# Router logits from four 32-column groups of the array, with the weights stationary

## The chip, the cores and the metric

The kernel runs on one core of one Trainium2 chip. The metric is the device time of one execution in microseconds. The engines are named as in the profile: PE is the matrix engine's products, PEld its weight loads, DVE the vector engine, ACT the scalar engine, POOL the general-purpose engine, and SP the engine whose queue issues most DMA transfers.

## The reference

One transformer block over 1024 tokens of width 1024, batch 1, float32. The mixing half feeds the residual stream; the second half routes tokens to experts. What the change touches is the router, the line of `aff`:

```
x = x + g1 * mixed                                  # (1024, 1024)
h2 = rmsnorm(x, norm_ffn_g) * (1.0 + sc2) + sh2
aff = softmax(h2 @ w_router)                        # (1024, 16)
g, idx = top_k(aff.T, cap)                          # 16 experts, 128 tokens each
...                                                 # gate, up, silu, down for each expert
x = x + g2 * scatter_add(...)
```

## The kernel before

The kernel has three stages. The first computes the modulation and the input projection. The second runs windowed attention and the Fourier branch, and beside them, as filler, the output projection. The third runs the experts, whose weights stream in.

Tokens are handled in eight tiles of 128 rows. `oproj(t)` makes the residual stream `x2` of tile `t` from the output projection (three float32r products per pair of slices: `mm3`, L81 to L83, into `pj` or, for the last two tiles, `lg`). It then hands over to `tail(t)`, a generator that runs while the next tile is projected:

- `x2_flip` (L826, L827) transposes `x2` on PE, four 128x128 blocks into a PSUM tile `pt`, and ACT copies them to `x2T`. Two flips make a tile: `x2T[:, kc, :]` holds 128 channels by 128 tokens, for eight slices `kc`.
- L837 forms the logits: eight products, one for each `kc`, that accumulate `p[tokens, 16]`. The tokens `x2T[:, kc, :]` are stationary (128 columns), and the router's weights `wrG[:, kc, :]` move past them, 16 columns wide.
- DVE scales and shifts them (`lg`, L839), takes the maximum (`mx`, L841), ACT makes the exponentials (`ex`, L844), and DVE normalises (L846, L847) into `aff`. A sorter on DVE picks thresholds from `aff` while later tiles run.

`router_prep` computes once `wrG`, the router's weights times the norm's scale (L866), and `cb`, the constant that the shift contributes.

The output projection is spread over attention's units. In the profile L685 and L686 are attention's logits, L688 their eviction on DVE, L697 the exponentials on ACT, L714 the transposes of the probabilities, L716 their copy `pT` on ACT, L727 the products with the values (`yp`, 64 columns of the array each, two halves of 64), and L660 the transposes of the queries.

`pt()` gives one of two PSUM buffers that flips, probability transposes, query transposes and the router share. A new use waits until the one before last has been read.

The order of instructions on each engine comes from a scheduler that places them by its own estimates, except where `in_order` pins a stretch to program order. This second stage isn't pinned. The last tile's tail, L800 to L847 near 405 to 413 us, has nothing of the output projection left beside it; the selection of the first expert's tokens (`choose`, L1141 to L1178), the one-hot rows (L1242), the gather of tokens (L1250, L1259) and the first expert's products (L1228) follow.

In the first stage `part_row` (L127) already uses column groups: a stationary tile of 32 columns, `c_act[:, j, :]`, writes partitions `32 * g` to `32 * g + 32` of a PSUM tile, with `g` going round four groups, and 256 or 512 columns of weights move past it. `mod_sum` then copies the tile with ACT (L253) and sums the groups with products against ones (L255).

Of the kernel before, what the change touches and what calls it, by code (L numbers as in the profile page):

```python
# [11 lines left out]
F32 = mybir.dt.float32  # L12
# [3 lines left out]
AF = mybir.ActivationFunctionType  # L16
OP = mybir.AluOpType
AX = mybir.AxisListType
# [7 lines left out]
NE = 16  # L26
# [19 lines left out]
def block_kernel(ctx: ExitStack, tc: tile.TileContext, t_in, out):  # L46
    nc = tc.nc
    PE, ACT, DVE, POOL, SP = nc.tensor, nc.scalar, nc.vector, nc.gpsimd, nc.sync
# [7 lines left out]
    def pool(name, bufs=1, space=None, **kw):  # L56
        if space is None:
            return tc.tile_pool(name=name, bufs=bufs, reuse_waits="tile", **kw)
        return tc.tile_pool(name=name, bufs=bufs, space=space, **kw)
# [4 lines left out]
    def spacer(p, n):  # L64
        if n:
            p.tile([128, n // 4], F32, name=f"spacer{next(spaced)}", bufs=1)
# [6 lines left out]
    def pt(name="pt"):  # L73
        return ps.tile([128, 512], F32, name=name, tag="pt", bufs=2)
# [18 lines left out]
    ident = cst.tile([128, 128], F32, name="ident")  # L93
# [47 lines left out]
    def drain(g):  # L141
        for _ in g:
            pass
# [202 lines left out]
    p = pt()  # L346
# [20 lines left out]
    def terms(ts, kc, hs_, o):  # L367
        for l, r in ((0, w_h), (1, w_h), (0, w_l)):
            for s_ in range(len(ts)):
                lhs = hs_[l][:, o + s_ * 128:o + s_ * 128 + 128]  # L370
                for acc, c0, c1 in zip(accs[s_], (0, 512, 1024), (512, 1024, 1280)):

                    first = kc == 0 and l == 0 and r is w_h and not (s_ and c0 == 1024)
                    PE.matmul(acc[:, :c1 - c0], lhs, r[kc][:, c0:c1], start=first, stop=(kc == 7 and r is w_l),  # L374
                              skip_group_check=c0 == 1024)
            yield
# [60 lines left out]
    p = terms(pair, 0, hs.pop(0), 0)  # L437
# [62 lines left out]
    for m, (t, kc0) in enumerate(seq):  # L500
# [20 lines left out]
        for a in range(4):  # L521
            project((t,), kc0 + a, hs_, a * 128)
            if m == 0 and a == 1:
                DVE.scalar_tensor_tensor(gg, qg, HD ** -0.5, kg, op0=OP.mult, op1=OP.mult)
                p = pt()
# [295 lines left out]
    def x2_flip(t, b, x2):  # L821
        if b == 0:
            x2Ts[t] = p3.tile([128, 8, 128], F32, name="x2T", bufs=1)
        p = pt()
        for k in range(4):
            PE.transpose(p[:, k * 128:k * 128 + 128], x2[:, (4 * b + k) * 128:(4 * b + k + 1) * 128], ident)  # L826
        ACT.activation(x2Ts[t][:, 4 * b:4 * b + 4].rearrange("p a b -> p (a b)"), p, AF.Copy)  # L827

    def tail(t, b0=0):
        x2, rs = x2s.pop(t)  # L830
        for b in range(b0, 2):
            x2_flip(t, b, x2)
            yield
        x2T = x2Ts.pop(t)
        p = pt()
        for kc in range(8):
            PE.matmul(p[:, :16], x2T[:, kc, :], wrG[:, kc, :], start=(kc == 0), stop=(kc == 7))  # L837
        lg = p3.tile([128, 16], F32, name="lg", bufs=2)
        DVE.scalar_tensor_tensor(lg, p[:, :16], rs, cb, op0=OP.mult, op1=OP.add)  # L839
        mx = p3.tile([128, 1], F32, name="mx", bufs=2)  # L840
        DVE.tensor_reduce(mx, lg, axis=AX.X, op=OP.max, negate=True)  # L841
        sm = p3.tile([128, 1], F32, name="sm", bufs=2)
        ex = p3.tile([128, 16], F32, name="ex", bufs=2)
        ACT.activation(ex, lg, AF.Exp, bias=mx, accum_out=sm)  # L844
        rsm = p3.tile([128, 1], F32, name="rsm", bufs=2)
        DVE.reciprocal(rsm, sm)  # L846
        after["aff"] = DVE.tensor_scalar(aff[:, t, :], ex, rsm, None, op0=OP.mult)  # L847
        ready.append(t)
        yield

    def router_prep():
        n2 = p3.tile([64, 128], F32, name="sb_", bufs=1)[:24]
        SP.dma_start(n2[0:8], md[1:2, :].rearrange("l (j p) -> (l j) p", p=128))
        SP.dma_start(n2[8:16], md[2:3, :].rearrange("l (j p) -> (l j) p", p=128))
        SP.dma_start(n2[16:24], t_in["norm_ffn_g"].rearrange("l (j p) -> (l j) p", p=128))
        p = pt()
        PE.transpose(p[:, :24], n2, ident[:24, :24])
        c2 = p3.tile([128, 24], F32, name="c2")
        DVE.tensor_copy(c2, p[:, :24])
        DVE.scalar_tensor_tensor(c2[:, 8:16], c2[:, 8:16], 1.0, c2[:, 16:24], op0=OP.add, op1=OP.mult)  # L860
        p = pt()
        for kc in range(8):
            PE.matmul(p[0:1, :16], c2[:, kc:kc + 1], wr[:, kc, :], start=(kc == 0), stop=(kc == 7))
        row = p3.tile([1, 16], F32, name="row")
        DVE.tensor_copy(row, p[0:1, :16])
        DVE.tensor_tensor(wrG, wr, c2[:, 8:16, None].to_broadcast([128, 8, 16]), op=OP.mult)  # L866
        p = pt()
        PE.matmul(p[:, :16], ones[0:1, :128], row, start=True, stop=True)
        DVE.tensor_copy(cb, p[:, :16])
# [65 lines left out]
    def wo_cut():  # L935
        k, j = divmod(next(wo_next), 2)
        split(wo_h[k][:, j], wo_l[k][:, j], wo_raw[k][:, j])
# [29 lines left out]
    po, p3 = None, None  # L967
# [18 lines left out]
    for n in range(len(units) + 2):  # L986
        if n == NSW:
            for _ in fill[0]:
                for g in lateq:
                    next(g, None)  # L990
            for g in lateq:
                drain(g)
            p_f.close()
            p_u.close()
            po = p_c.enter_context(pool("po"))
            p3 = p_c.enter_context(pool("p3", side="right"))
            sp[0] = p3
            spacer(p3, 0)
            g1_r, sh2_r, G2_r = (p3.tile([128, D], F32, name=n_) for n_ in ("g1_r", "sh2_r", "G2_r"))
            wr, wrG = (p3.tile([128, 8, NE], F32, name=n_) for n_ in ("wr", "wrG"))  # L1000
            cb = p3.tile([128, NE], F32, name="cb")
            load_x2(0)
            for i, r in enumerate((g1_r, sh2_r, G2_r)):
                SP.dma_start(r, md[i:i + 1, :].to_broadcast([128, D]))
            wo_h.append(po.tile([128, 2, D], F32R, name="woh3"))
            wo_l.append(po.tile([128, 2, D], F32R, name="wol3"))
            wo_cut()
            wo_cut()
            fill = [filler2()]
            SP.dma_start(wr, t_in["w_router"][0].rearrange("(k p) e -> p k e", p=128))  # L1010
        fg = front(*units[n]) if n < len(units) else iter(())
        bg = back(*units[n - 2]) if n >= 2 else iter(())
        next(fg, None)
        next(bg, None)
        next(fg, None)
        next(bg, None)
        next(bg, None)
        drain(fg)
        for g in lateq:
            for _ in range(9):  # L1020
                next(g, None)
        if n + 1 < len(units):
            qprep(*units[n + 1])
            tick()
        drain(bg)
# [277 lines left out]
    for b in range(2):  # L1303
        p = pt()
# [120 lines left out]
```

## Time and profile before

| what | value |
|---|---|
| median of 3 runs | 1007.59 us (1006.1 to 1008.08) |
| profiled execution, its own time | 1009.72 us |
| its span, first to last instruction | 1007.6 us |
| mean granted clock of PE | 0.971 |
| instructions | 13138 |
| PE busy | 949.8 us (94%) |
| DVE busy | 788.1 us (78%) |
| ACT busy | 627.8 us (62%) |
| POOL busy | 404.7 us (40%) |

A row of a timeline has the start and the duration in us, the engine, the line of the kernel, the operation, output and inputs by their names in the program, for PE the rows and columns of the stationary tile that are in use, the shape that moves, and how many such instructions follow each other; in brackets stands the idle time ahead of it and what ended it. A float32 product shows as two records of PE, each with a weight load of its own. A row of the chain of work has start, duration, engine, output and line. Times of a group are its total and the mean of one in ns. In a list of waits the three numbers are the total, the times, and the longest.

### The profile page before, as it was taken

The page shows a single profiled execution, that of the slowest core. Times are in us where ns is not written, and L with a number is a line of the kernel's source. Part 1 is how long each engine was busy: PE and PEld are TensorE (multiplying, and loading weights), DVE is VectorE, ACT ScalarE, POOL GpSimd, SP SyncE. Part 2 cuts the span into 40 slices and gives each one's busy share as a digit, 9 for nine tenths or more (in the row PEclk, how much of TensorE's full clock was granted, in tenths as well). Part 3 has the DMA queues.
Part 4 walks back from the last instruction along what each step waited for, and adds up shares of the span by engine and source line. Part 5 has one row for each costly group of instructions (what it writes and reads, how often), then busy time and mean ns, then how long its engine had stood idle before and what let it go on. Part 6 is the DMA issues. An engine that isn't in the chain of part 4 may idle for free.

```text
span 1007.6 us, 13138 instructions
## 1 busy us (share of the span) xinstructions
PE 949.8 (94%) x4737; PEld 747.4 (74%) x4737; DVE 788.1 (78%) x1240; ACT 627.8 (62%) x832; POOL 404.7 (40%) x236
## 2 busy tenths in 40 slices
PE   4997999979999999499899999999999999999995
PEld 2675877657777778358788888888888888888884
DVE  1346874787667787879869889988988898899894
ACT  2473533656555552136767777778777777777872
POOL 0025552200000000000257678769766976882203
PEclk9998999989999999599989999999999999999998
DMA  9967582461222228799989999999999999999912
GB/s 291 328 246 251 209 313 83 134 183 47 98 84 74 74 84 289 314 335 355 390 343 359 385 396 399 387 385 409 388 389 385 411 385 389 404 392 387 386 68 42
DMA packets 91641, 283.95 MB, mean 282 GB/s; under 512 B 8140, under 2 KB 25728, under 8 KB 91448
## 3 DMA queue, kind: packets, MB, share of 16 engines
q1 hardware_dynamic: 86712, 266.32, 69.5%
q0 software_dynamic: 4864, 16.80, 6.5%
q8 instruction: 37, 0.61, 0.2%
q14 instruction: 28, 0.23, 0.1%
HBM read 263.79 MB, written 21.40 MB: 283 GB/s over the span
## 4 chain that ended last, share of the span: by engine, by line
PE 83%; DVE 6%; POOL 3%; issue 2%; ACT 2%; DMA 1%; SPq 1%; POOLq 0%; ACTq 0%
PE pa L81 17%; PE pa L82 16%; PE pa L83 16%; PE pu L374 5%; PE yp L727 3%; PE pt L1269 3%; PE pj L81 2%; PE pj L82 2%; PE pt L714 2%; PE pj L83 2%; PE pa L1228 2%; PE pt L837 2%; PE lg L685 1%; DVE ws L123 1%; PE lg L686 1%
## 5 line engine op out<-in xcount | busy, mean ns | idle before, releaser
L87 DVE TENSOR_TENSOR wl<-raw,wh 128x2048 fp32r<-128x2048 f32 (+1 forms) x189 | 424.2, 2275 | 56.0 <-ACT wh L86 54.9
L86 ACT ACTIVATE wh<-raw 128x2048 fp32r<-128x2048 f32 (+1 forms) x189 | 355.4, 1896 | 73.7 <-PE pa L82 65.8
L1242 POOL TENSOR_SCALAR oneh<-tri_f,pos 128x128 bf16<-128x128 f32 x96 | 210.5, 2207 | 15.1 <-PE pt L1250 14.8
L81 PE MATMUL pa<-wh,t1h 128*128 128x512 f32 x384 | 151.4, 394 | 0.0
L83 PE MATMUL pa<-wl,t1h 128*128 128x512 f32 x384 | 149.5, 389 | 0.0
L82 PE MATMUL pa<-wh,t1l 128*128 128x512 f32 x384 | 149.5, 389 | 0.0
L81 PE MATMUL pa<-wh,t0h 128*128 128x512 f32 x360 | 143.5, 399 | 0.0
L82 PE MATMUL pa<-wh,t0l 128*128 128x512 f32 x360 | 141.1, 392 | 0.0
L83 PE MATMUL pa<-wl,t0h 128*128 128x512 f32 x360 | 141.1, 392 | 0.0
L800 POOL TENSOR_TENSOR rs<-ss,mhalf 128x1 f32<-128x1 f32 x8 | 4.5, 558 | 221.3 <-DVE ss L798 194.4
L1284 POOL TENSOR_TENSOR ys<-ys,g_r 128x512 f32<-128x512 f32 x30 | 54.5, 1837 | 84.9 <-ACT ys L1283 84.9
L83 PEld LDWEIGHTS pa<-wl,t1h 128*128 128x128 f32 x384 | 72.1, 188 | 15.1
L82 PEld LDWEIGHTS pa<-wh,t1l 128*128 128x128 f32 x384 | 72.2, 188 | 14.2
L81 PEld LDWEIGHTS pa<-wh,t1h 128*128 128x128 f32 x384 | 72.1, 188 | 14.2
L83 PEld LDWEIGHTS pa<-wl,t0h 128*128 128x128 f32 x360 | 68.1, 189 | 14.5
L81 PEld LDWEIGHTS pa<-wh,t0h 128*128 128x128 f32 x360 | 68.3, 190 | 13.7 <-issue 0.2
L82 PEld LDWEIGHTS pa<-wh,t0l 128*128 128x128 f32 x360 | 68.2, 190 | 13.6 <-issue 0.2
L1259 POOL DMA_INDIRECT xe<-h2d,idx x16 | 18.7, 1171 | 147.3 <-DVE gt L1256 147.2
L1287 POOL DMA_INDIRECT out_dram<-ys,idx x16 | 50.8, 3174 | 10.9 <-DVE ys L1286 6.4
L688 DVE CUSTOM_DVE_ANT_0 sb<-lg,bias,sink 128x384 f32<-128x384 f32 (+1 forms) x64 | 35.3, 579 | 17.4 <-PE pt L714 9.8
L278 ACT ACTIVATE hf<-pt,sh1c,G1c 128x128 f32<-128x128 f32 (+1 forms) x56 | 22.6, 480 | 38.7 <-PE pt L271 38.7
L374 PE MATMUL pu<-wh,hh 128*128 128x512 f32 x128 | 43.6, 423 | 2.3 <-ACT hh L86 2.2
(311 smaller groups left out, 1649.0 us busy)
## 6 DMA issues: line engine op xcount, KB each, us to landing
raw<-in_w_gate_dram SPq DMA_DIRECT2D x64, 1024.0 KB, 10.0
raw<-in_w_up_dram SPq DMA_DIRECT2D x64, 1024.0 KB, 8.5
raw<-in_w_down_dram SPq DMA_DIRECT2D x63, 1024.0 KB, 8.6
raw<-in_w_ada_dram SPq DMA_DIRECT2D x16, 1024.0 KB, 8.6
raw<-in_w_ada_dram SPq DMA_DIRECT2D x16, 512.0 KB, 8.7
xt<-in_x_dram SPq DMA_DIRECT2D x8, 512.0 KB, 5.0
raw<-in_w_out_dram SPq DMA_DIRECT2D x4, 1024.0 KB
raw<-in_x_dram SPq DMA_DIRECT2D x8, 512.0 KB
```

What stands on the lines that cost most here:

```text
L81: PE.matmul(o, lh, rh, start=start, stop=False)
L82: PE.matmul(o, ll, rh, start=False, stop=False)
L83: return PE.matmul(o, lh, rl, start=False, stop=stop)
L86: ACT.activation(hi, src, AF.Copy)
L87: return (eng or DVE).tensor_tensor(lo, src, hi.bitcast(F32), op=OP.subtract)
L374: PE.matmul(acc[:, :c1 - c0], lhs, r[kc][:, c0:c1], start=first, stop=(kc == 7 and r is w_l), skip_group_check=c0 == 1024)
L688: DVE.tensor_tensor_reduce(sb[:, :wid], lg[:, :wid], bias[:, kv * 4 + i, j0:j0 + wid], 1.0, sk[:, i:i + 1], op0=OP.add, op1=OP.max, accum_ ...
L727: PE.matmul(yp[par * 64:par * 64 + 64, :256], vf[:, b, kv * 64:kv * 64 + 64], pT[:, par * 256:par * 256 + 256], start=(bi == 0), stop=(bi ...
L1242: (POOL if t < shared else DVE).tensor_scalar(oneh[:, t, :], slots, pos[:, t, e:e + 1], None, op0=OP.is_equal)
L1269: PE.transpose(p[:, k * 128:k * 128 + 128], src[:, (4 * b + k) * 128:(4 * b + k + 1) * 128], ident)
L1284: POOL.tensor_tensor(ys[:, cs_], ys[:, cs_], g2_r[:, cs_], op=OP.mult)
L1287: POOL.indirect_dma_start(out=out2, out_offset=bass.IndirectOffsetOnAxis(ap=idx[:, :1], axis=0), in_=ys, in_offset=None, compute_op=OP.add)
```

## The change

The two operands of the router's product trade places. The weights `wrG[:, kc, :]`, widened with zeros from 16 to 32 columns, are stationary in column group `kc % 4`, and the 128 tokens of `x2T[:, kc, :]` move past them. The eight products leave four partial sums in `p`, group `g` (slices `g` and `g + 4`) in partitions `32 g` to `32 g + 32`, with experts down the partitions and tokens along the row. ACT copies `p` to a tile `gsum` in SBUF. One product with `gsum` stationary and `gsel` moving, where `gsel[p, e]` is one if `p % 32 == e`, sums the four groups and turns the result back to 128 tokens by 16 experts. `gsel` is made once on DVE, by adding up the four 32-column blocks of the identity; `wrG` is zeroed once on POOL.

```diff
@@ tail(t)
         x2T = x2Ts.pop(t)
+
         p = pt()
         for kc in range(8):
-            PE.matmul(p[:, :16], x2T[:, kc, :], wrG[:, kc, :], start=(kc == 0), stop=(kc == 7))
+            g = 32 * (kc % 4)
+            PE.matmul(p[g:g + 32, :128], wrG[:, kc, :], x2T[:, kc, :], start=(kc < 4), stop=(kc >= 4))
+        gs_ = p3.tile([128, 128], F32, name="gsum", bufs=1)
+        ACT.activation(gs_, p[:, :128], AF.Copy)
+        p = pt()
+        PE.matmul(p[:, :16], gs_, gsel[:, :16], start=True, stop=True)
         lg = p3.tile([128, 16], F32, name="lg", bufs=2)
@@ router_prep
-        DVE.tensor_tensor(wrG, wr, c2[:, 8:16, None].to_broadcast([128, 8, 16]), op=OP.mult)
+        DVE.tensor_tensor(wrG[:, :, :NE], wr, c2[:, 8:16, None].to_broadcast([128, 8, 16]), op=OP.mult)
@@ setting up the second part of stage two
-            wr, wrG = (p3.tile([128, 8, NE], F32, name=n_) for n_ in ("wr", "wrG"))
+            wr = p3.tile([128, 8, NE], F32, name="wr")
+            wrG = p3.tile([128, 8, 32], F32, name="wrG")
+            gsel = p3.tile([128, 32], F32, name="gsel")
+            POOL.memset(wrG, 0.0)
+            DVE.tensor_reduce(gsel, ident.rearrange("p (g e) -> p e g", g=4), axis=AX.X, op=OP.add)
```

In the changed file the eight products are L839, the copy is L841, the summing product L843, and `lg`, `mx`, `ex` become L845, L847, L850. In the rows below, a product's operands are written output, moving, stationary, and the shape is the stationary columns by the moving ones.

The scheduler places the rest of the second stage anew. On PE, around the router of the third tile (tile 2), the two halves of the product came apart before and stand together now:

```order
 L826 MATMUL pt<-ident,raw 128x128 x4
 L727 MATMUL yp<-pT,vf 64x256
-L837 MATMUL pt<-wrG,x2T 128x16 x4
+L839 MATMUL pt<-x2T,wrG 32x128 x8
 L727 MATMUL yp<-pT,vf 64x256
 L82 MATMUL pj<-woh_1523,yal 128x512
-L837 MATMUL pt<-wrG,x2T 128x16 x4
+L83 MATMUL pj<-wol_1526,yah 128x512
+L843 MATMUL pt<-gsel,gsum 128x16
 L714 MATMUL pt<-ident,sb 128x128 x4
```

Half of L727, L82 and L83 stand between the grouped product and the summing product.

On PE, around the router of the second tile (tile 1), before:

```order
L714 MATMUL pt<-ident,sb 128x128 x4
L837 MATMUL pt<-wrG,x2T 128x16 x8
L727 MATMUL yp<-pT,vf 64x256 x2
L714 MATMUL pt<-ident,sb 128x128 x4
L82 MATMUL pj<-woh_1523,yal 128x512
```

and of the change:

```order
L82 MATMUL pj<-woh_1523,yal 128x512
L839 MATMUL pt<-x2T,wrG 32x128 x8
L727 MATMUL yp<-pT,vf 64x256
L843 MATMUL pt<-gsel,gsum 128x16
L727 MATMUL yp<-pT,vf 64x256
L714 MATMUL pt<-ident,sb 128x128 x4
```

The summing product has moved in between the two halves of L727. Of the other tiles, tiles 2 and 3 have a half of L727 on each side of the grouped product, tile 6 has another product between the first four and the last four of L839, and in tiles 0, 4, 5 and 6 two or three products stand between L839 and L843.

On DVE, in the last tile's tail, the second half of the norm's shift (L806) stood behind `lg` and now stands ahead of it. Before:

```order
L805 SCALAR_TENSOR_TENSOR raw<-raw,rs,G_r 128x512
L839 SCALAR_TENSOR_TENSOR lg<-pt,rs,cb 128x16
L806 TENSOR_TENSOR raw<-raw,sh_r 128x512
L841 TENSOR_REDUCE mx<-lg 128x1
L846 RECIPROCAL rsm<-sm 128x1
```

and of the change:

```order
L805 SCALAR_TENSOR_TENSOR raw<-raw,rs,G_r 128x512
L806 TENSOR_TENSOR raw<-raw,sh_r 128x512
L845 SCALAR_TENSOR_TENSOR lg<-pt,rs,cb 128x16
L847 TENSOR_REDUCE mx<-lg 128x1
L852 RECIPROCAL rsm<-sm 128x1
```

L806 has moved up by one row, so `lg` and all that depends on it come behind it.

On ACT at the same place, a cut of expert weights (L86, `wh`) stood behind the last flip's copy; all four such cuts now stand ahead of it, and the copy to `gsum` follows it directly:

```order
L86 ACTIVATE wh<-raw 128x1024 x4
L793 ACTIVATE junk,ss<-raw 128x512
L827 ACTIVATE x2T<-pt 128x512
L841 ACTIVATE gsum<-pt 128x128
L850 ACTIVATE ex,sm<-lg,mx 128x16
```

The fourth cut has moved ahead of the flip, and nothing stands between the copies `x2T`, `gsum` and the exponentials.

## The prediction

> **What bounds the kernel now.** I read the page's busy line first, then three stretches of the span, then the chain of work over the stretch that the router lies in.
>
> ```profile
> PE 949.8 (94%) x4737; PEld 747.4 (74%) x4737; DVE 788.1 (78%) x1240; ACT 627.8 (62%) x832; POOL 404.7 (40%) x236
> ...
> 225.00:404.00 179.00, 178.60 (x1010) 132.35 (x1009) 133.49 (x468) 96.77 (x267) 4.53 (x9) 0.99 0.30 108
> 404.00:427.00 23.00, 10.47 (x56) 8.10 (x56) 19.73 (x80) 3.87 (x8) 2.36 (x3) 0.56 0.78 305
> 427.00:1000.00 573.00, 566.34 (x2687) 460.99 (x2686) 503.61 (x452) 418.75 (x313) 331.25 (x156) 0.99 0.95 359
> ```
>
> The columns of a stretch are its length, then busy time of PE, PEld, DVE, ACT and POOL, the granted clock, the DMA share and GB/s. From 225 to 404 us PE is busy 178.60 of 179 us at a clock of 0.99; DVE has 133 us of work and ACT 97, so both have room. Here seven of the eight router tails run. From 404 to 427 DVE is the busy one (19.73 of 23) and PE has half its clock: the last tail and the first selection. After that PE is the bound again. The chain agrees:
>
> ```profile
> by line: PE yp L727 13.9%; PE pj L81 12.7%; PE pj L82 12.2%; PE pj L83 12.0%; PE pt L714 11.5%; PE pt L837 6.9%; PE lg L685 4.9%; PE lg L686 4.1%; PE pt L826 3.4%; PE lg L81 3.2%; PE lg L82 3.2%; PE lg L83 3.1%; PE pt L660 2.2%; DVE sc L879
> ...
> 278.41 1.79 PE pt L837 x16
> ...
> 407.54 3.24 PE pt L837 x16
> ```
>
> The first row is the chain's share by line from 225 to 404 us. L837, the router product, holds 6.9% of 179 us, so 12.35 us for seven tiles, 1.76 each. That is 16 records of 0.11 us (1.79/16): each product is two records. The eighth takes 3.24 us at half clock.
>
> ```profile
> L837 PEld LDWEIGHTS pt<-wrG,x2T x112: 186/192/192, 258.3 to 396.0; 128*128 128x128 f32 x112
> L837 PE MATMUL pt<-wrG,x2T x112: 177/263/283, 258.5 to 396.1; 128*128 128x16 f32 x112
> ```
>
> Each record loads 128 columns of tokens to move 16 columns of weights past them. The load sets the 0.11 us, not the moving side. That is what the swap attacks.
>
> **Removed.** Tails 0 to 6: 12.35 us of PE, all of it on the path, since PE has no slack there.
>
> **Added: the grouped product (L839).** In the text L839 to L843 are lines of the changed file; in the profile's rows L839 is lg and L841 mx. Before has the same form in L127: 32 columns stationary, four groups in turn, float32.
>
> ```profile
> 48.97 0.63 PE L374 MATMUL pu<-wh,hl 128*128 128x512 f32 x2
> 49.44 0.28 PE L374 MATMUL pv<-wh,hl 128*128 128x256 f32 x1
> 49.65 1.92 PE L127 MATMUL px<-raw,c_act 128*32 128x512 f32 x16
> 51.50 0.73 PE L374 MATMUL pu<-wl,hh 128*128 128x512 f32 x2
> ...
> 49.65 0.16 PEld L127 LDWEIGHTS px<-raw,c_act 128*32 128x32 f32 x8 [0.25 <-issue]
> 50.10 0.13 PEld L127 LDWEIGHTS px<-raw,c_act 128*32 128x32 f32 x4 [0.30 <-issue]
> 50.53 0.13 PEld L127 LDWEIGHTS px<-raw,c_act 128*32 128x32 f32 x4 [0.30 <-issue]
> ```
>
> Eight products, 16 records, go in four bursts; the loads of the later ones start 0.43 us apart (50.10, 50.53). So four records run side by side in 0.43 us for 512 columns. 128 columns are a quarter, 0.11 a burst, 0.43 for four. The visit has a fixed part: 51.50 - 49.65 - 4 x 0.43 = 0.13 inside, 0.10 more on the next row (0.73 against 0.63), and 0.09 ahead (49.44 to 49.65 is 0.21 for 256 columns, where 512 take 0.235, half of 48.97 to 49.44); together 0.32. So 0.75 if loads hide wholly. A load of 32 columns takes as long as the shorter burst, so they may hide in part; 0.85 is my upper value, and I take 0.80, nearer to the rows as they stand.
>
> **Added: the summing product (L843).** A 128-column load and 16 moving columns, exactly L837's form: two records, 0.22 us. Seven tiles of 0.80 + 0.22 make 7.14 us.
>
> **Added: places where the order splits a visit.** L727 uses 64 columns of the array.
>
> ```profile
> 302.76 0.65 PE L727 MATMUL yp<-pT,vf 128*64 128x256 f32 x2
> 303.33 1.06 PE L837 MATMUL pt<-wrG,x2T 128*128 128x16 f32 x8
> 304.33 0.65 PE L727 MATMUL yp<-pT,vf 128*64 128x256 f32 x2
> 304.90 0.50 PE L82 MATMUL pj<-woh,yal 128*128 128x512 f32 x1
> ...
> 280.13 0.65 PE L727 MATMUL yp<-pT,vf 128*64 128x256 f32 x4
> 280.71 0.66 PE L714 MATMUL pt<-ident,sb 128*128 128x128 f32 x4
> ```
>
> Four records together take 0.58 us (280.13 to 280.71); two alone take 0.57 as well (302.76 to 303.33). In tile 1 the summing product now stands between L727's halves, which stood together: +0.57. Tiles 2 and 3 had them apart and keep that. Tile 6 has L839 in two visits: +0.32. Elsewhere the new order shuffles attention and output-projection rows but adds none; I price that at nothing, since PE's rows stay the same and PE always had a next one.
>
> **Added: the wait for the copy (L841).** PE cannot issue past the summing product while it waits, so all of PE's queue stands behind it.
>
> ```profile
> L385 ACT ACTIVATE kk<-pv 128x128 f32<-128x128 f32 x5 | 1.4, 285 | 0.0
> ...
> 301.67 0.66 PE L714 MATMUL pt<-ident,sb 128*128 128x128 f32 x4
> 302.43 0.60 ACT L716 ACTIVATE pT<-pt 128x512 f32<-128x512 f32 x1 [0.31 <-PE pt L714]
> ...
> 298.43 0.39 PE L83 MATMUL pj<-wol,yh 128*128 128x512 f32 x1
> 298.66 0.39 PE L81 MATMUL pj<-woh,yh 128*128 128x512 f32 x1
> ```
>
> The copy is 0.29 us (L385, same shape, from PSUM); PE's end to ACT's start is 0.10 (302.33 to 302.43). With L839's own tail (0.16: the records of L83 and L81 last 0.39 at a spacing of 0.23) and a hand-back that I put at half of ACT's 0.10, 0.60 us pass. The cover is what the order puts between: in tiles 2 and 3 half of L727 and two products, over 1 us; in tiles 0, 4, 5 and 6 two or three products, 0.56 or more with the 0.10 of leaving the visit; in tile 1 half of L727, with two pT copies of 0.60 ahead in ACT's queue. I allow 0.1 for six tiles and 0.3 for tile 1: 0.9, between zero and 0.60 each (4.2). ACT itself is early:
>
> ```profile
> ACT pT L716 <- PE pt L714: 27.6, 23, 3.5
> ```
>
> From 225 to 400 us ACT waited 27.6 us for PE in 23 places ahead of pT alone.
>
> **Sum for tiles 0 to 6:** 7.14 + 0.57 + 0.32 + 0.9 = 8.93 added, 12.35 removed, 3.42 us gained. Prologue: the memset of wrG has the size of c_act's, 0.31 us on POOL; the reduction to 32 elements lies between the next two DVE rows by elements read, near 0.3 us. Neither engine is on the path there; zero. The wider wrG holds the same 16 written columns; zero.
>
> ```profile
> L107 POOL MEMSET c_act<- 128x256 f32 x1 | 0.3, 312 | 0.3 <-POOLq L1414 0.3
> L290 DVE TENSOR_REDUCE qs<-ws 128x10 f32<-128x640 f32 x8 | 6.5, 814 | 2.9 <-ACT ws L288 2.9
> L841 DVE TENSOR_REDUCE mx<-lg 128x1 f32<-128x16 f32 x8 | 1.3, 162 | 0.1
> ```
>
> **The last tile** is latency:
>
> ```profile
> 407.33 3.43 PE L837 MATMUL pt<-wrG,x2T 128*128 128x16 f32 x16
> 407.57 0.60 ACT L827 ACTIVATE x2T<-pt 128x512 f32<-128x512 f32 x1
> 408.07 1.05 ACT L86 ACTIVATE wh<-raw 128x1024 fp32r<-128x1024 f32 x1
> 408.89 0.75 DVE L805 SCALAR_TENSOR_TENSOR raw<-raw,rs,G_r 128x512 f32<-128x512 f32 x1 [0.75 <-POOL rs L800]
> 410.80 0.23 DVE L839 SCALAR_TENSOR_TENSOR lg<-pt,rs,cb 128x16 f32<-128x16 f32 x1 [1.16 <-PE pt L837]
> 410.95 0.68 DVE L806 TENSOR_TENSOR raw<-raw,sh_r 128x512 f32<-128x512 f32 x1
> 411.55 0.16 DVE L841 TENSOR_REDUCE mx<-lg 128x1 f32<-128x16 f32 x1
> ```
>
> L837's records take 0.21 here (3.43/16), twice 0.11, so I double L839's prices. Its first half, two bursts and the entry, ends near 408.4. The second needs x2T (408.17): 0.43 of streaming and a tail of 0.35, near 409.2. The copy, behind which the wh cut of 408.07 no longer stands in front, ends at 409.6; the sum takes 0.43 and a tail of 0.35: 410.4. DVE now does L806 before lg: L805 ends at 409.64, L806 at 410.32, so lg starts at 410.4 and mx at 410.6 instead of 411.55: 0.95 gained. DVE and the selection behind wait for that.
>
> **Total:** 3.42 + 0.95 = 4.4 us, on the profiled execution's own 1009.72 (span 1007.6) as on the median, which lies 2.1 below it: 1007.59 - 4.4 = 1003.2. What would give it back is late next:
>
> ```profile
> PE pt L1250 <- DVE t1l L87: 3.6, 1, 3.6
> ACT wh L86 <- DMA raw<-in_w_gate_dram: 2.7, 3, 1.2
> ```
>
> From 425 us on PE waits once, 3.6 us, for DVE's one-hot rows, and ACT 2.7 us for weights. Selection, gather and reloads all start from the router's result or from freed buffers, so I let them move along whole.
>
> **Bounds.** Best: L839 at 0.68 (a visit at L727's 0.25 instead of 0.33), the splits at 0.82, no waits: 7.12 added, 5.2 gained, and 1.05 on the last tile if lg starts as L806 ends: 1001.3. The lowest run lies 1.5 below the median; half of that makes 1000.6. Worst of the forecast: every wait 0.60 instead of the 0.9 together costs 3.3 more, 1006.5.
>
> **Rivals.**
> - *The loads do not hide.* Each burst would be a load and then its streaming, 0.11 + 0.11: L839 takes 0.88 + 0.32 = 1.20, 0.40 more, 2.8 on seven tiles and 0.4 on the last by its one late half at half clock: gain 1.2, 1006.4. For it: no row shows bursts as short as their loads. Against it: in L127 all eight loads of the first two bursts issue within 0.16 us, the second four under the first burst's streaming. Chance 0.10. [...]
> - *Slower: the copy comes late in ACT's queue.* If two rows as long as pT (0.60) stand ahead of it, unfinished when L839 ends, PE waits 1.2 us in each of seven tiles: 8.4 - 4.3 - 0.95 = +3.1, 1010.7. It decides at 0.75 us a tile, a little over one such row. For it: ACT is in order and 54% busy (96.77 of 179). Against: the new order puts the copy right behind x2T or pT. Chance 0.08.
> - *The groups do not run side by side,* so the change does not do what it says: 16 x 0.11 + 0.32 + 0.22 = 2.3 a tile against 1.76, +3.8, with splits and waits +5.6, and nothing on the last tile: near 1013. L127's bursts speak against it. Chance 0.04.
> - *The gain is lost behind 404 us,* in the 3.6 us wait of L1250 or the weights: 1006.5 to 1007.6. Chance 0.10.
>
> **Chances.** Forecast 0.68, faster. Runs tell 0.2%, 2 us, from nothing: unhidden loads and the loss behind 404 count as same, 0.20; the two slower rivals 0.12. The range runs from the best case with scatter, 1000.6, past unhidden loads to 1007.3; the forecast alone has 1000.6 to 1005.5.
>
> **What would show it.** L839 as 16 records in four bursts of 0.11 to 0.13 us, a tail's PE time near 1.0 us instead of 1.76; PE waits on the copy below 1 us in total; mx of the last tile 4.4 us earlier (near 407.1); the wait at L1250 still about 3.6 us. Bursts of 0.22, waits on the copy of 0.7 a tile, or a longer wait at L1250 would make the prediction wrong, each by its rival.

## The result, and the profile after

| | before | changed |
|---|---|---|
| median | 1007.84 us (6 runs, 1004.64 to 1011.92) | 999.65 us (6 runs, 996.11 to 1001.56) |
| profiled execution, its span | 1009.72, 1007.6 us | 1001.56, 999.6 us |
| granted clock of that execution | 0.971 | 0.971 |

The ratio is 0.9905, with a 95% interval from 0.9883 to 0.9927: faster by 8.2 us in the medians. The forecast was 4.4 us, 1003.2, with a range from 1000.6 to 1007.3. The sign was right, the size a little over half, and the result lies just outside the range.

The busy line of the changed kernel, and the same three stretches shifted to its own stages (columns: length, busy time of PE, PEld, DVE, ACT and POOL, granted clock, DMA share, GB/s):

```profile
PE 943.3 (94%) x4753; PEld 736.5 (74%) x4753; DVE 788.5 (79%) x1241; ACT 630.2 (63%) x840; POOL 404.3 (40%) x237
...
225.00:395.50 170.50, 170.08 (x1020) 121.57 (x1019) 133.59 (x468) 98.95 (x274) 4.47 (x9) 1.00 0.31 114
395.50:418.50 23.00, 9.26 (x66) 5.79 (x65) 20.53 (x83) 4.34 (x9) 2.36 (x3) 0.58 0.80 311
418.50:991.50 573.00, 567.14 (x2687) 461.22 (x2684) 502.89 (x449) 418.66 (x313) 331.13 (x156) 0.99 0.95 359
```

The first of them still keeps PE full; the other two, cut as long as before, hold about the same work (PE 567.1 us against 566.3 in the last). The last product of the output projection starts at 395.80 us instead of 404.06, so 8.3 us are gained ahead of the last tile. `mx` is 9.1 us earlier, the end 8.0: what the last tile adds is given back behind it.

The new instructions, by groups (count, total and mean in ns, idle time ahead and what ended it):

```profile
L839 PE MATMUL pt<-x2T,wrG 128*32 128x128 f32 x128 | 6.2, 298 | 0.2
...
L839 PEld LDWEIGHTS pt<-x2T,wrG 128*32 128x32 f32 x128 | 2.8, 112 | 3.6 <-issue 1.2 <-ACT x2T L827 1.2 <-ACT pT L716 1.1
L843 PEld LDWEIGHTS pt<-gsel,gsum 128*128 128x128 f32 x16 | 2.8, 203 | 2.0 <-ACT gsum L841 1.7
...
L843 PE MATMUL pt<-gsel,gsum 128*128 128x16 f32 x16 | 2.7, 247 | 0.4 <-ACT gsum L841 0.4
...
L841 ACT ACTIVATE gsum<-pt 128x128 f32<-128x128 f32 x8 | 2.2, 278 | 4.4 <-PE pt L839 4.4
```

Eight tails of grouped products keep PE busy for 6.2 us. PE itself waited 0.4 us for the copy, once, in the last tile; the 1.7 us are waits of the load queue. Tile 1 in the timeline:

```profile
276.42 0.64 PE L839 MATMUL pt<-x2T,wrG 128*32 128x128 f32 x16
277.00 0.65 PE L727 MATMUL yp<-pT,vf 128*64 128x256 f32 x2
277.57 0.39 PE L843 MATMUL pt<-gsel,gsum 128*128 128x16 f32 x2
277.90 0.65 PE L727 MATMUL yp<-pT,vf 128*64 128x256 f32 x2
```

The next row starts 0.58 us after L839 and 0.33 after L843. The 16 records in 0.58 us fit the four bursts of 0.11 that were forecast.

The last tile:

```profile
395.80 0.39 PE L83 MATMUL lg<-wol,yah 128*128 128x512 f32 x1
...
398.67 0.66 PE L826 MATMUL pt<-ident,raw 128*128 128x128 f32 x4 [2.49 <-DVE raw L791]
...
401.06 0.61 PE L843 MATMUL pt<-gsel,gsum 128*128 128x16 f32 x2 [0.40 <-ACT gsum L841]
...
401.60 0.69 DVE L806 TENSOR_TENSOR raw<-raw,sh_r 128x512 f32<-128x512 f32 x1
402.21 0.23 DVE L845 SCALAR_TENSOR_TENSOR lg<-pt,rs,cb 128x16 f32<-128x16 f32 x1
402.47 0.17 DVE L847 TENSOR_REDUCE mx<-lg 128x1 f32<-128x16 f32 x1
```

From the last flip's first product to `mx` it is 3.80 us (398.67 to 402.47) at a granted clock of 0.57: 0.50 from 399.2 us on. `lg` waits for L806, not for the sum. `mx` was forecast 4.4 us earlier than in the profile before and came 9.1 us earlier; the other 4.7 us came in ahead of this tile.

### The profile page after: what moved, and what is told of

Read it like the earlier page. It is cut to its first block, busy times and chain, and to the rows that moved or that the text cites. A ratio compares the mean times of both kernels' runs of the same rounds, so it can differ in the third digit from the quotient of the medians.

```text
span 999.6 us, 13182 instructions
## 1 busy us (share of the span) xinstructions
PE 943.3 (94%) x4753; PEld 736.5 (74%) x4753; DVE 788.5 (79%) x1241; ACT 630.2 (63%) x840; POOL 404.3 (40%) x237
## 4 chain that ended last, share of the span: by engine, by line
PE 82%; DVE 7%; POOL 3%; issue 2%; ACT 2%; DMA 1%; SPq 1%; POOLq 0%; ACTq 0%; DVEq 0%
PE pa L81 17%; PE pa L83 17%; PE pa L82 17%; PE pu L374 5%; PE yp L727 3%; PE pt L1279 3%; PE pj L82 2%; PE pj L81 2%; PE pj L83 2%; PE pt L714 2%; PE pa L1238 2%; PE lg L685 1%; PE lg L686 1%; DVE ws L123 1%; DVE wl L87 1%
## 5 line engine op out<-in xcount | busy, mean ns | idle before, releaser
L86 ACT ACTIVATE wh<-raw 128x2048 fp32r<-128x2048 f32 (+1 forms) x189 | 355.3, 1896 | 74.1 <-PE pa L82 66.9
L81 PE MATMUL pa<-wh,t1h 128*128 128x512 f32 x384 | 151.4, 394 | 0.0
L83 PE MATMUL pa<-wl,t1h 128*128 128x512 f32 x384 | 149.6, 390 | 0.0
L82 PE MATMUL pa<-wh,t1l 128*128 128x512 f32 x384 | 149.5, 389 | 0.0
L81 PE MATMUL pa<-wh,t0h 128*128 128x512 f32 x360 | 143.8, 399 | 0.0
L83 PE MATMUL pa<-wl,t0h 128*128 128x512 f32 x360 | 141.2, 392 | 0.0
L82 PE MATMUL pa<-wh,t0l 128*128 128x512 f32 x360 | 141.2, 392 | 0.0
L83 PEld LDWEIGHTS pa<-wl,t1h 128*128 128x128 f32 x384 | 72.1, 188 | 15.1
L82 PEld LDWEIGHTS pa<-wh,t1l 128*128 128x128 f32 x384 | 72.2, 188 | 14.2
L81 PEld LDWEIGHTS pa<-wh,t1h 128*128 128x128 f32 x384 | 72.1, 188 | 14.2
L83 PEld LDWEIGHTS pa<-wl,t0h 128*128 128x128 f32 x360 | 68.2, 189 | 14.5
L82 PEld LDWEIGHTS pa<-wh,t0l 128*128 128x128 f32 x360 | 68.4, 190 | 13.7 <-issue 0.2
L81 PEld LDWEIGHTS pa<-wh,t0h 128*128 128x128 f32 x360 | 68.3, 190 | 13.7 <-issue 0.2
L1269 POOL DMA_INDIRECT xe<-h2d,idx x16 | 18.7, 1170 | 146.8 <-DVE gt L1266 135.6
L688 DVE CUSTOM_DVE_ANT_0 sb<-lg,bias,sink 128x384 f32<-128x384 f32 (+1 forms) x64 | 35.4, 580 | 15.6 <-PE pt L714 7.9
```

The source lines that it names most:

```text
L81: PE.matmul(o, lh, rh, start=start, stop=False)
L82: PE.matmul(o, ll, rh, start=False, stop=False)
L83: return PE.matmul(o, lh, rl, start=False, stop=stop)
L86: ACT.activation(hi, src, AF.Copy)
L688: DVE.tensor_tensor_reduce(sb[:, :wid], lg[:, :wid], bias[:, kv * 4 + i, j0:j0 + wid], 1.0, sk[:, i:i + 1], op0=OP.add, op1=OP.max, accum_ ...
```

## The experiments

Two theories stood at the start: A, the 8 us are array time taken off PE in the tails; B, a good part comes from the scheduler laying the stage anew. A third, C, came from one stretch of the profile before:

```profile
328.00:331.00 3.00, 3.00 (x20) 2.08 (x18) 1.42 (x2) 0.83 (x2) 0.00 (x0) 1.00 0.24 97
331.00:335.00 4.00, 4.00 (x16) 2.46 (x16) 0.80 (x4) 0.40 (x2) 0.00 (x0) 0.61 0.52 189
335.00:338.00 3.00, 3.00 (x18) 2.02 (x17) 2.83 (x12) 1.49 (x4) 0.00 (x0) 0.95 0.03 5
```

Right behind the fourth tile's L837, PE is granted 0.61 of its clock for 4 us: 1.56 + 0.15 us lost, so 3.4 us at half clock. The changed kernel has 1.00 in this stretch.

### The setup alone, and the order it makes

The changed kernel's setup (wide `wrG`, `gsel`) with the old product:

```diff
-            PE.matmul(p[g:g + 32, :128], wrG[:, kc, :], x2T[:, kc, :], ...)   # and the copy and the sum
+            PE.matmul(p[:, :16], x2T[:, kc, :], wrG[:, kc, :NE], start=(kc == 0), stop=(kc == 7))
```

> The changed kernel's setup alone (the zeroed, 32-wide wrG, the reduction to gsel), with the old product on the 16 written columns. Theory A, PE's account: the 8.2 us come from array time taken off PE in seven tiles (the trace after has 12.25 us of L837 replaced by 4.44 of L839 and 1.32 of L843, so 6.5) and from the last tile (0.8); the setup is worth nothing, so this run lies within 1.5 us of the kernel before (1007.8). Theory B, placement: about half of the gain comes from the scheduler laying the second stage anew once instructions are added; then this run, whose order also changes, lies 2 to 4 us below, near 1004.

Measured: 1006.12 us, ratio 0.9981 (0.9963 to 1.0). That is too near to no change to decide by itself. The same kernel once more:

> The setup alone once more, to see whether its 2.0 us hold. Theory B, placement: again 1.5 us or more below the kernel before. Theory A: the two results together lie within 1.5 us of the kernel before.

Measured: 1005.61 us, ratio 0.9973 (0.9956 to 0.999). Over both runs the 24 executions average 2.2 us below 103 of the kernel before, give or take 0.9 (two standard errors). A setup that computes nothing on the critical path makes the kernel faster: theory B holds for a part. The kernel before, unchanged, beside it:

> The kernel before, unchanged, for a second profiled execution and a control of the comparison. [...] Time: within 0.2% of itself.

Measured: 1008.84 us, ratio 0.9997 (0.9975 to 1.0018), and no half-clock stretch between 225 and 400 us (granted 1.00 from 254.7 to 400.3). So C's stretch was an accident of one execution, and this second profile is the better one to compare with. PE at the start of the second stage, in the kernel before as profiled again:

```profile
215.38 0.63 PE L81 MATMUL pj<-woh,yh 128*128 128x512 f32 x1
216.97 0.79 PE L82 MATMUL pj<-woh,yl 128*128 128x512 f32 x1 [0.96 <-DVE yl L87]
...
218.41 0.63 PE L82 MATMUL pj<-woh,yl 128*128 128x512 f32 x1
218.84 0.52 PE L685 MATMUL lg<-khi,qk 128*128 128x384 f32 x1
```

and with the setup alone, second run:

```profile
215.03 0.63 PE L81 MATMUL pj<-woh,yh 128*128 128x512 f32 x1
215.46 0.63 PE L82 MATMUL pj<-woh,yl 128*128 128x512 f32 x1
...
218.28 0.40 PE L82 MATMUL pj<-woh,yl 128*128 128x512 f32 x1
218.51 0.39 PE L83 MATMUL pj<-wol,yh 128*128 128x512 f32 x1
218.75 0.34 PE L685 MATMUL lg<-khi,qk 128*128 128x384 f32 x1
```

Between L81 and L685 there are 4 products of the output projection in the first (the dots stand for two) and 11 in the second (the dots stand for eight), the later of them at full clock (0.23 us from row to row), and L685 starts at the same time. Seven products of 0.23 us, 1.6 us, have moved into a gap of PE from the path behind 243 us. They can, because DVE delivers `yl`, the low part of their operand, sooner. DVE in the kernel before:

```profile
214.55 1.23 DVE L87 TENSOR_TENSOR wol<-raw,woh 128x1024 fp32r<-128x1024 f32 x1
...
216.22 0.69 DVE L87 TENSOR_TENSOR yl<-yt,yh 128x512 fp32r<-128x512 f32 x1
```

and with the setup:

```profile
214.20 0.38 DVE L1005 TENSOR_REDUCE gsel<-ident 128x32 f32<-128x128 f32 x1
214.50 0.69 DVE L87 TENSOR_TENSOR yl<-yt,yh 128x512 fp32r<-128x512 f32 x1
```

With the reduction of `gsel` in front of it, the scheduler puts `yl` ahead of a weight cut (`wol`) and of an eviction (L688, 0.61 us from 215.69 before, 0.62 us from 215.27 with the setup). Three runs test that it is this reduction. First the setup without it:

```diff
-            DVE.tensor_reduce(gsel, ident.rearrange("p (g e) -> p e g", g=4), axis=AX.X, op=OP.add)
```

> The kernel before with wrG widened and zeroed, without the reduction to gsel; PE's planned order is that of the kernel before. Theory B, as now told: the setup's 2 to 2.7 us came from the place of the reduction on DVE, so this run shows no change (within 1 us). If the memset or the wider tile were behind it: 2 us faster.

Measured: 1007.84 us, ratio 0.9998 (0.9981 to 1.0016): no change. Then the whole change with the reduction moved:

```diff
@@ setting up the second part of stage two
-            DVE.tensor_reduce(gsel, ident.rearrange("p (g e) -> p e g", g=4), axis=AX.X, op=OP.add)
@@ the end of router_prep
         DVE.tensor_copy(cb, p[:, :16])
+        DVE.tensor_reduce(gsel, ident.rearrange("p (g e) -> p e g", g=4), axis=AX.X, op=OP.add)
```

> The changed kernel with one thing moved: the reduction that makes gsel stands at the end of router_prep instead of ahead of the loads. The planned order then has 6 products of the output projection ahead of the second unit's logits, as the kernel before has, and not 13. Theory B, as the traces now show it: with the early reduction seven such products (1.6 us) fill a gap of PE near 220 us, and without it they lie on the path behind 243 us. So this run gives back 1.6 to 2.5 us: 1001 to 1002, and lies 5.5 to 6.5 below the kernel before, which is the product's own share. If the order there is worth nothing: 999.5, as the changed kernel.

Measured: 1003.11 us, ratio 0.9951 (0.9931 to 0.997). `yl` stands behind the weight cut and the eviction there again, and PE waits for it. From the list of waits:

```profile
PE pj L82 <- DVE yl L87: 1.5, 1, 1.5
```

The profile before had this very row, word for word; in the changed kernel the wait is 0.2 us. Once more, beside the changed kernel:

> The changed kernel with the reduction at the end of router_prep, once more, beside the changed kernel. The order near 220 us accounts for 1.6 us by the rows of seven products, and for up to 3.6 by the medians so far (1003.11 against 999.5). Expected 1.6 to 3.6 us above the changed kernel.

> The changed kernel, unchanged, as the measure for the runs with filler and with the late reduction in the same rounds: 999.3 to 999.7, as twice before.

Measured: 1000.83 us (0.9946, 0.9925 to 0.9967) against 998.91 (0.9921, 0.9892 to 0.9951). Over all runs the product alone, with the reduction late, averages 6.0 us (give or take 1.0) below the kernel before, and the changed kernel 3.0 (1.3) below that. Seven products explain 1.6 of these 3.0.

The profiles show more. The stretch from the transposes ahead of these products (the first L714) to the first copy to `x2T` holds this order and nothing of the router, and PE has the same 217 records there in either order. In the kernel before (as profiled again), and then with the setup alone, second run:

```profile
213.19:254.73 41.54, 40.38 (x217) 28.38 (x218) 32.92 (x101) 27.10 (x78) 0.56 (x1) 0.92 0.36 114
```

```profile
212.84:252.13 39.29, 39.09 (x217) 27.67 (x218) 33.01 (x102) 27.36 (x78) 0.56 (x1) 0.96 0.37 120
```

PE idles 0.20 us instead of 1.16, and the granted clock is 0.96 instead of 0.92, so the half clock at the start of the stage lasts about half as long: 3.1 us instead of 6.6, by estimate from 0.04 of 39.29 and 0.08 of 41.54 us. The stretch took 41.2 to 42.2 us in the seven profiles with the old order (clock 0.92 in six of them) and 38.4 to 40.0 in the thirteen with the new one (0.96 in twelve), 2.1 us less in the mean. That the filled gap is what shortens the half clock was not tested by a run of its own. What is left of the 3.0 lies within the error.

### What the product itself is worth

The stage from the first copy to `x2T` to the last product of the output projection holds the tails 0 to 6 and nothing of the gap or the last tile. One window over that stage in each kernel's profile, the kernel before (as profiled again):

```profile
254.70:400.30 145.60, 145.20 (x826) 109.03 (x824) 107.99 (x389) 74.35 (x203) 3.96 (x8) 1.00 0.33 118
```

the changed kernel:

```profile
255.90:395.80 139.90, 139.48 (x839) 100.31 (x838) 108.05 (x389) 76.40 (x209) 3.92 (x8) 1.00 0.34 124
```

and the change with the late reduction:

```profile
257.90:398.10 140.20, 139.73 (x839) 100.31 (x838) 107.73 (x389) 76.47 (x210) 3.92 (x8) 1.00 0.34 124
```

At full clock the stage is as good as a stopwatch: 145.1 to 145.6 us in the five profiles with the old product at full clock, 139.9 to 140.3 in the nine with the new one. So the product gains 5.3 us in seven tiles. The parts of it, by further runs:

| kernel | stage, us | |
|---|---|---|
| old product, undisturbed | 145.3 | |
| changed | 139.9 | |
| changed, without copy and sum | 137.5 | 2.45 less |
| changed, one column group | 149.5 | 9.6 more |
| changed, products twice | 142.95 | 3.05 more |
| old, first of eight products | 135.6 | 9.7 less than old |

The run without copy and sum reads `lg` from the first partial sums:

```diff
-        gs_ = p3.tile([128, 128], F32, name="gsum", bufs=1)
-        ACT.activation(gs_, p[:, :128], AF.Copy)
-        p = pt()
-        PE.matmul(p[:, :16], gs_, gsel[:, :16], start=True, stop=True)
```

> The grouped product without the copy and without the summing product: lg reads partition p, columns 0 to 15, of the partial sums, so the routing is that of other numbers; the rest of the work keeps its shape. Theory A: the copy costs only the array time of L843 (1.32 us over seven tiles), 0.4 us of waits, and on the last tile about 0.6: 2.3 us below the changed kernel, near 997.4. By the prediction's sizes (0.22 each, waits of 0.9, the split of L727 at 0.57, 0.8 on the last tile) it would be 3.8 us below, near 995.9. A price of 5 us or more would say that the copy's wait holds PE in most tiles.

Measured: 997.59 us, ratio 0.9883 (0.9849 to 0.9916). The stage says 0.35 a tile for copy, sum, split and waits together. One column group:

```diff
-            PE.matmul(p[g:g + 32, :128], ..., start=(kc < 4), stop=(kc >= 4))
+            PE.matmul(p[:32, :128], ..., start=(kc == 0), stop=(kc == 7))
...
-        ACT.activation(gs_, p[:, :128], AF.Copy)
+        ACT.activation(gs_[:32], p[:32, :128], AF.Copy)
-        PE.matmul(p[:, :16], gs_, gsel[:, :16], start=True, stop=True)
+        PE.matmul(p[:, :16], gs_[:32], ident[:32, :16], start=True, stop=True)
```

> The changed kernel with all eight products in one column group (partitions 0 to 32, one accumulation), the copy of 32 partitions and the summing product with 32 rows. Same loads, same streaming, nothing side by side. Theory A, the four groups overlap: 16 records of 0.11 us instead of four bursts of 0.11, so 1.32 us more in each of seven tiles (9.2) and 0.8 on the last: 10 us above the changed kernel, near 1009.7. Rival: the groups do not matter, since it is the loads of 32 columns instead of 128 that shortened the product; then within 2 us of the changed kernel.

Measured: 1009.83 us, ratio 1.0019 (1.0002 to 1.0036). Without concurrency the whole gain is gone. The products twice:

```diff
-        for kc in range(8):
+        for kc in 2 * list(range(8)):
```

> The changed kernel with the eight grouped products issued twice in the same visit. Theory A: four more bursts of 0.11 us in seven tiles, 3.1, and 0.4 to 0.8 on the last: 3.5 to 3.9 above the changed kernel, near 1003.3. If L839 were hidden beside other work: no change. If the loads did not hide: twice as much, near 1007.

Measured: 1002.17 us, ratio 0.9934 (0.9911 to 0.9957). Tile 1's product shows both, first with one group (L838 there), then twice (the changed kernel's L839 has 0.64 for 16 records):

```profile
274.35 1.93 PE L838 MATMUL pt<-x2T,wrG 128*32 128x128 f32 x16
```

```profile
275.04 1.08 PE L839 MATMUL pt<-x2T,wrG 128*32 128x128 f32 x32
```

Four more bursts cost 0.44 us, 0.11 each, and a load of 32 columns takes 0.11 by itself (112 ns in the groups above), so their loads hide. Twelve more take 1.29. The first product alone:

```diff
-        for kc in range(8):
-            PE.matmul(..., start=(kc == 0), stop=(kc == 7))
+        for kc in range(1):
+            PE.matmul(..., start=(kc == 0), stop=(kc == 0))
```

> The kernel before with the first of the eight products alone, so the logits hold one slice of 128 channels and the routing is that of other numbers. Theory A: 14 of 16 records gone from seven tiles, 10.7, and 1.3 on the last tile, where the next limit is the wait for rs: 12 below the kernel before, near 996. If the gain of the change is bounded elsewhere, it stops near 999.7.

Measured: 1000.78 us, ratio 0.9918 (0.9897 to 0.9939), where 996 was expected: a miss. The stage has its 9.7 us (expected 10.7), but the medians only 7.3. Its last tile is no faster (7.1 us from the last product to `mx`, 7.5 in the profile before), and from the last product to the end it takes 605.3 us, near the longest of the old tail (602.8 to 605.5 in six profiles). The rest of the miss is not explained. Less its two records, 0.22 a tile, a stage without any router product is 134.1 us, by estimate. So the old product cost 11.2 us in seven tiles, the grouped one 3.4, and the rest of the new tail 2.45.

Tiles 0 to 6 and tile 7 apart:

```diff
-        p = pt()
+        if t < NT - 1:      # and in the other run: t == NT - 1
+            ...             # the grouped product, copy and sum
+        else:
+            ...             # the old product
```

> The grouped product in tiles 0 to 6, the old one in tile 7. Theory A: 6.5 us gained on PE and none on the last tile: about 1001.3, and this gain and that of the run with the last tile alone add up to the 8.2 us of the whole change within 1.5. The prediction's own sizes would give 3.4, so 1004.4. Theory B: gains do not add up by tiles.

> The grouped product in tile 7 alone. Theory A, and the prediction: 0.8 to 1.0 us gained between the end of the output projection and the maximum, so about 1006.9, which is hardly told from no change. Theory B: 2 to 4 us, from placement, as for the setup alone.

Measured: 999.69 us (0.9911, 0.9879 to 0.9943) and 1005.68 us (0.9977, 0.9958 to 0.9996). Both hold the setup. Less its 2.2 us, the early tiles bring 6.2 and the last one 0.3, neither told from 5.3 and 0.95.

### The clock

The old product twice:

```diff
-        for kc in range(8):
+        for kc in 2 * list(range(8)):
```

> The kernel before with its eight products L837 issued twice. Theory A, a price by array time alone: 16 records of 0.11 in seven tiles, 12.3, and up to 3.4 on the last at half clock: 13 to 16 above the kernel before, near 1022. Theory C, the clock: the product moves 16 columns for every 128 that it loads, and the granted clock falls to half for 3.4 us after a stretch of it (the trace before has one such stretch at 331 to 335 us, right behind the fourth tile's product, and none there after the change); then twice the product brings such stretches in more tiles, 1.7 us each, seen in the granted clock between 225 and 404 us, and the time goes to 1025 or above.

Measured: 1035.07 us, ratio 1.0275 (1.024 to 1.0311): theory C's number. Tile 1 of this kernel, and the granted clock about tiles 1 and 3:

```profile
277.59 3.74 PE L837 MATMUL pt<-wrG,x2T 128*128 128x16 f32 x32
...
281.84 1.03 PE L714 MATMUL pt<-ident,sb 128*128 128x128 f32 x4
```

```profile
280.00:285.00 5.00, 5.00 (x28) 3.18 (x28) 2.02 (x8) 0.60 (x1) 0.00 (x0) 0.70 0.62 213
...
335.00:340.00 5.00, 5.00 (x37) 3.99 (x36) 1.76 (x2) 1.09 (x2) 0.00 (x0) 1.00 0.25 105
340.00:345.00 5.00, 5.00 (x17) 3.28 (x17) 0.80 (x4) 0.40 (x2) 0.00 (x0) 0.50 0.31 105
...
254.50:424.90 170.40, 170.21 (x938) 130.21 (x936) 108.68 (x391) 74.47 (x202) 3.96 (x8) 0.92 0.28 101
```

After 3.7 us of 16-column products, L714's four records take 1.03 us instead of 0.66. The stage is 25.1 us longer than the undisturbed one. At a clock of 0.92, 0.08 of 170.4, or 13.6 us, are lost to it; 11.5 are left, 1.6 a tile, the old product's price again. So a stretch of these products does bring the half clock, though PE counts as busy throughout. In its single form it did so in one of the six profiles with the old product in all seven tiles, so for the 8 us it counts little. Idle time in PE's rows does not account for it: PE was busy 3.00 of 3.00 us ahead of the stretch in the profile before, and 3.70 of 3.70 from 278 to 281.7 us in this kernel. What in these products brings it was not shown.

Does a busier PE bring the clock back in the selection, where it is half (granted 0.50) from 399.2 to 423.1 us? Two bundles of products that nobody reads:

```diff
@@ choose(e), behind the two transposes of aff
+        if e == 1:
+            for _ in range(12):
+                PE.matmul(p[:, 256:512]..., ones_b, tri..., start=True, stop=True)   # 256 columns, bfloat16
@@ behind the product with edge
+        if e == 1:
+            for _ in range(12):
+                PE.matmul(pe[:, 256:512]..., ones_b, tri..., start=True, stop=True)
```

> The changed kernel with two bundles of 12 products that nobody reads (tri against ones_b, 256 columns, bfloat16) in two gaps of PE during the selection of the second expert's tokens, 411.7 to 414.3 and 415.5 to 418.3 us in the trace after. If the half clock of 399 to 423 us is kept up by PE's gaps, PE is back at full clock by about 419 instead of 423 us, and the first expert's products (5.0 us for 8 records of L1238 at half clock) lose some 2 us less: 1.5 to 2.5 us below the changed kernel, near 997.7. If the gaps do not set the clock, or the filler holds up the selection: no gain, or up to 1 us slower.

Measured: 998.79 us, ratio 0.9905 (0.9883 to 0.9928), no gain that can be told. The half clock did end earlier: it lasted 20.5 us, from 394.8 to 415.3, instead of 23.9. But the selection's comparisons read the same PSUM tile as the filler's first bundle and waited for it: from the transposes of `aff` to the product with `kept` 4.59 us passed, instead of 3.84 in the changed kernel. With a tile of its own for that bundle (`pf = pa()`):

> The two bundles of filler again, with the first writing to a PSUM tile of its own, so that the comparisons that read the selection's tile do not wait for it. In the run before, the filler ended the half clock 3.4 us earlier and held the selection up by 0.8. Without that wait the gain at the first expert's products is about 1.8 us: 997.5 to 998. If the first bundle's wait was not what held it: 998.8, as before.

Measured: 995.64 us, ratio 0.9878 (0.9858 to 0.9899). And beside the changed kernel:

> The changed kernel with the two bundles of filler, the first in its own PSUM tile, once more, beside the changed kernel. The run before gave 995.64. [...]

Measured: 995.68 us, ratio 0.9899 (0.987 to 0.9927), against 998.91. Over both runs that is 3.1 us (give or take 1.3) below the changed kernel, more than the 1.8 expected at first. The traces agree: from `mx` to the end the changed kernel takes 596.9 to 597.2 us in its three profiles, and this version 594.1 and 594.2. This is the version that beats both. The selection's end and the first expert's products, in the changed kernel and then in this one:

```profile
418.67 1.95 PE L1316 MATMUL pt<-ident,xe 128*128 128x128 f32 x8
420.45 5.01 PE L1238 MATMUL pa<-raw,ys 128*128 128x512 f32 x8
```

```profile
410.95 2.72 PE L1186 MATMUL pa<-tri,ones_b 128*128 128x256 bf16 x12
414.00 0.19 PE L1130 MATMUL pa<-gq,tri 128*128 128x12 bf16 x1 [0.33 <-DVE gq L1144]
...
414.34 1.07 PE L1325 MATMUL pt<-ident,xe 128*128 128x128 f32 x8
415.66 3.70 PE L1247 MATMUL pa<-raw,ys 128*128 128x512 f32 x8 [0.25 <-ACT ys L1326]
```

The transposes take 1.07 instead of 1.95 us and the first eight products 3.70 instead of 5.01, so these two rows hold 2.2 us of the gain.

The last control, the changed kernel beside the setup alone:

> The changed kernel, unchanged, beside the setup alone and the kernel before in the same rounds. By the stage times of the profiles so far (145.1 to 145.4 us with the old product at full clock, 139.9 with the new) the product itself is worth 5.3 us in tiles 0 to 6 and 0 to 0.8 on the last, so it lies 5.3 to 6.1 us below the setup alone, and the rest of the 8.2 below the kernel before is the setup's share and the clock's. Should it lie 8 us below the setup alone, the product explains the whole.

Measured: 999.31 us, ratio 0.9901 (0.9875 to 0.9926), 6.3 us below the setup alone. The product does not explain the whole.

## Why the prediction was right in kind and short in size

**The step that failed:** "Elsewhere the new order shuffles attention and output-projection rows but adds none; I price that at nothing, since PE's rows stay the same and PE always had a next one." PE had a next one from 225 us on (busy 178.60 of 179 us), but not ahead of that. The first product with `yl`, before and then after:

```profile
219.55 0.80 PE L82 MATMUL pj<-woh,yl 128*128 128x512 f32 x1 [1.55 <-DVE yl L87]
```

```profile
218.33 0.79 PE L82 MATMUL pj<-woh,yl 128*128 128x512 f32 x1 [0.17 <-DVE yl L87]
```

Behind this wait PE ran 4 products of the output projection ahead of the next logits (L685), and now it runs 11. The seven rows that the new order moved from a full stretch into a gap are gone from the path. I had read windows from 225 us only, and the wait of 1.5 us for `yl`, in the list of waits, was left out. It was worth 1.6 us by the rows, 2.1 by the stretch from the transposes to the first copy to `x2T`, and 2 to 3 by the times, and nothing in the sum stood for it, nor in any rival.

Between the two profiles the 8.3 us ahead of the last tile divide so: the stage took 147.1 us before and 139.9 after, 7.2 less, of which 1.7 are the half-clock stretch of that one execution; the first copy to `x2T` comes 1.1 us earlier. The stretch ahead of that copy took 41.2 us before and 39.9 after: the profile before is the one of the old order in which the half clock there was as short as in the new, so this pair shows the order's gain only in part.

**The term that was mis-sized:** the grouped product at 0.80 us, of which 0.32 was the fixed part of a visit. The fixed part that the whole stage shows is 0.05 (3.4 us / 7 less four bursts of 0.11), by the estimate of the empty stage. L839's visit does take 0.58 us in tile 1, 0.14 more than its bursts; but it stands where PE switches shapes anyway, and may take over a cost that was there; no run tested that. Read off three rows around an isolated visit, the fixed part came out 0.27 us larger than by the stage, and the neighbours' own switches may be counted in it.

| term, tiles 0 to 6 | forecast | measured by the stage |
|---|---|---|
| L837 removed | 12.35 | 11.2 |
| L839, with tile 6's split | 5.92 | 3.4 |
| sum, L727's split, waits for the copy | 3.01 | 2.45 |
| net gain | 3.42 | 5.3 |

- L837's share of the chain was 1.1 us more than leaving it out saves; it may be the same in reverse, its neighbours' switches remaining, which was not tested. That its loads set the 0.11 us agrees with the rows: in tile 1 of the profile before, PEld is busy with them for 1.86 of the visit's 1.89 us (278.24 to 280.13).
- The waits for the copy: below 1 us, as foretold, and on PE's side 0.4 us.
- The last tile: forecast 0.95. From the last product to `mx` it took 7.49 us before and 6.67 after, 0.82 less. From the last flip on it is 1.08 less (4.88 to 3.80); 0.26 of that go to small rows of DVE that now stand ahead of the flip. `lg` came behind L806 and not behind the sum. But where the half clock set in later (L837's 16 records took 1.92 us in the kernel before as profiled again, 2.53 with the setup alone, second run, and 3.43 in the profile before), the old tail took 6.2 to 6.4 us. From the last product to the end six profiles with the old tail have 602.8 to 605.5 us and six with the new one 602.8 to 603.9, 0.6 less in the mean, so this term can't be told from the scatter.
- Behind 404 us the forecast let the gain move along whole. L1250's wait (L1260 now) is 3.6 us as foretold, and the first expert's products start 9.1 us earlier, as `mx` does. But the half clock (granted 0.50 up to 423.1 us, before up to 430.9) lasts further into them, 2.7 us instead of 1.3, and the first eight take 5.01 us instead of 4.35. So 8.4 us are left behind them, and 8.0 at the end; the last 0.4 is left open.
- Loads: bursts of 0.11 us, in single and double form, where the first rival had 0.22, so they hide.
- Groups side by side: shown by 0.64 against 1.93 us.

With the reduction out of the way the changed kernel ran in 1003.11 and 1000.83 us. That the first is the predicted number is luck: the tiles gave 5.3 us where 3.4 were forecast, and the last tile's 0.95 can't be told from nothing.

## What to carry to other kernels

When a change adds an instruction anywhere ahead of an unpinned stage, compare the planned order outside the edit, and price rows that cross from a stretch where PE is full into one where it waits. Price a small product by leaving it out or doubling it in the stage, since a visit's entry and exit may be paid by whatever stands there (0.05 us a visit by the stage here, 0.32 by the rows). Where PE runs at half clock through a latency-bound stretch ahead of heavy products (granted 0.50 for 23.9 us here), filler that nobody waits for can pay: here it was worth 3.1 us (give or take 1.3), about a third of what the change itself was.

## What the runs showed that I had not expected

- Behind 3.7 us of products that move 16 columns the granted clock was half for about 3.4 us (tile 1 with L837 twice: 0.70 from 280 to 285 us, 0.96 from 285 to 290), with PE recorded as busy all along; L837 twice cost 25.1 us in the stage, of which 13.6 were the clock's.
- Four 32-column groups run side by side at no visible loss: 0.11 us a burst of four records.
- A reduction of 0.38 us on DVE, whose result nothing reads in the setup alone, made the kernel 2.2 us faster (give or take 0.9) by its place in the order.
- With that order PE filled a gap near 217 us, and the half clock there lasted about half as long: a clock of 0.96 over the stretch in twelve profiles of thirteen, where the old order had 0.92 in six of seven.
